# Gate and up projections of a feed-forward block as seven block products, activation kept in DRAM

## Chip, cores and metric

The kernel runs on one core of a Trainium2 chip. The metric is the device time of one launch in microseconds (us). The core has five engines with a queue of their own each, worked through in order: PE (matmuls, with PEld for the weight loads that run beside them), DVE (vector work), ACT (activations and copies), POOL (GpSimd), and SP, whose queue here only issues DMAs.

## What is computed

The program is one encoder layer: three token mixers, an output projection, a SwiGLU feed-forward block and a final norm, for 512 tokens of width 1024. The change touches the seam between output projection and feed-forward, the feed-forward itself, and the start of the down projection:

```python
x = x + merged @ w_out
h2 = rms_norm(x, g_ffn)
ffn = (jax.nn.silu(h2 @ w_ffn_gate) * (h2 @ w_ffn_up)) @ w_ffn_down
return rms_norm(x + ffn, g_final)
```

The gate and up weights are 1024 x 2816 each, the down weight is 2816 x 1024, all in float32.

## The kernel before

**Precision.** A float32 operand is held as a pair: `hi` is the value rounded to the matmul's input type by ACT, `lo` the rest, subtracted out by DVE. `split` does both. `mm3` makes three matmuls of one product: hi by hi, lo by hi, hi by lo. So every operand that a matmul reads costs one pass on ACT and one on DVE first. The DVE pass reads the raw value and `hi`: two inputs in SBUF, unless the raw value still lies in PSUM.

**Weights.** `wload` brings one weight tile of 128 x 1024 by a DMA on SP's queue into `raw` (2 buffers) and splits it into `w_hi` and `w_lo` (3 buffers).

**Seam.** The output projection ends token tile by token tile (four tiles of 128 tokens). After each, `to_h2` scales the normed rows into `xn`, PE transposes them (eight 128 x 128 transposes into two PSUM banks of `pt`, which has 2), and `transpose_split` splits them into `h2_hi`, `h2_lo`: two ACT passes and two DVE passes for each token tile.

**Gate and up.** The loop over `f` has 22 rounds of 128 columns of the feed-forward width. A round loads two tiles, from `w_fg` and `w_fu`, and makes 2 x 8 x 3 matmuls of 512 token columns, gate into a bank of `pg` (2 banks), up into one of `po` (4). The first two rounds are cut into two halves of 256 columns, so that they can begin when the first two token tiles are ready. Then ACT takes the tanh, DVE makes two passes, and a last split writes `act_hi[f]`, `act_lo[f]` in SBUF.

**Down.** `projection` runs over 11 chunks of two `f` for the low half of the output columns, then for the high half, with the tokens as the stationary side and the weights moving.

**Order.** The source is not the order that runs: a scheduler orders each engine's queue by its own model of time when the program is built, and fixes it there. Waits between engines are semaphores. Where a pool of buffers is released and another takes its room, the new tile's first writer waits for the old tile's last users.

Of the kernel before, what the change touches and what calls it, by code (L numbers as in the profile page):

```python
# [55 lines left out]
def block_kernel(ctx, tc, x, mem, pos, inv, g_mix, mem_g, g_ffn, g_final, g_q, g_kv, gate_bias,  # L56
# [37 lines left out]

    def mm3(ps, terms, start=True, stop=True):
        n = len(terms)
        for i, (wh, wl, ah, al) in enumerate(terms):
            mm(ps, wh, ah, start=start and i == 0, stop=False)  # L98
            mm(ps, wh, al, start=False, stop=False)  # L99
            mm(ps, wl, ah, start=False, stop=stop and i == n - 1)  # L100
# [11 lines left out]
    def transpose_split(pp, src, nk, hi, lo, t):  # L112
        for k0 in range(0, nk, 4):
            n = min(4, nk - k0)
            tp = pp.tile([P, 512], F32, name=pp.name, tag=pp.name)
            for k in range(n):
                nc.tensor.transpose(tp[:, k * P:(k + 1) * P], src[:, (k0 + k) * P:(k0 + k + 1) * P], ident)
            tv = tp[:, :n * P].rearrange("p (k c) -> p k c", k=n)
            split(hi[:, k0:k0 + n, t * P:(t + 1) * P], lo[:, k0:k0 + n, t * P:(t + 1) * P], tv)

    with ExitStack() as mix:
# [678 lines left out]
        hp = tc.alloc_tile_pool(name="hp", bufs=1, side="right")  # L800
        gff_b = hp.tile([P, D], F32, name="gff_b")
        bcast_rows(gff_b, g_ffn)
# [31 lines left out]

        def projection(banks, w, nch, tail, ah, al, hold, early, done):
            vs = []
            for half in range(2):
# [31 lines left out]
        def to_h2(t, r):  # L869
            xn = hp.tile([P, D], F32, name="xn", tag="xn", bufs=2)  # L870
# [27 lines left out]
    last = tc.alloc_tile_pool(name="last", bufs=1, side="right")
# [9 lines left out]
    def store(t, r):  # L908
# [4 lines left out]
        for c0 in range(H, D, n):  # L913
# [87 lines left out]
```

## Time and profile before

| what | value |
|---|---|
| time, median of 3 runs | 947.45 us (945.56 to 947.97) |
| profiled execution, span from first to last instruction | 944.7 us |
| PE busy in the span | 927.1 us |
| output projection | up to about 568 us of the span |
| gate and up projection | about 568 to 817 us |
| down projection, final norm and store | about 817 us to the end |

The page gives no time of the profiled execution but its span; the median lies 2.75 us above it. In the timeline a row is start, duration, engine, line, operation, output and inputs, and how many instructions were merged; idle time ahead of it stands in brackets with what ended it. Neighbouring matmuls overlap in these rows, so a matmul's cost is the distance between starts. In the table by stretches each engine has its busy time and its number of instructions, then the clock that PE was granted (1.00 is 2.4 GHz, 0.50 is 1.2 GHz), the DMA engines' share and GB/s.

### The profile page before, as it was taken

The numbers are of one execution on the slowest core, as the hardware profiler recorded it, in microseconds if no ns is written. First come the engines' busy times: TensorE is split into PE (matmuls) and PEld (weight loads), VectorE is DVE, ScalarE is ACT, GpSimd is POOL, SyncE is SP. The second block draws the span as 40 slices with busy tenths as digits, with TensorE's granted clock in tenths as the row PEclk, the third lists the DMA queues.
The fourth block names the chain that finished last, engine by engine and source line by source line (L and its number), as shares of the span: only waits on it lengthen the run. The fifth ranks groups of instructions, "written<-read, shape, count | busy, mean of one in ns | idle before, by whom it ended". The sixth has DMA issues, their size and how long they took to land.

```text
span 944.7 us, 12173 instructions
## 1 busy us (share of the span) xinstructions
PE 927.1 (98%) x4598; PEld 768.6 (81%) x4598; DVE 529.8 (56%) x909; ACT 448.1 (47%) x770; POOL 84.8 (9%) x139
## 2 busy tenths in 40 slices
PE   7998999999999999999999999999999999999997
PEld 5886887888888788888888889888888888888886
DVE  5678968788776756776556664433433334322322
ACT  8566667686653457677664342323222232212222
POOL 2000002212111110100004200000000000000200
PEclk9999999999999999999999999999999999999999
DMA  7521244434332032122225431332223222232222
GB/s 267 157 73 52 74 137 131 150 125 138 134 109 90 26 104 67 56 68 76 76 89 180 133 112 46 100 100 90 90 91 106 94 89 90 90 112 90 93 86 89
DMA packets 32058, 96.32 MB, mean 102 GB/s; under 512 B 4656, under 2 KB 7024, under 8 KB 32000
## 3 DMA queue, kind: packets, MB, share of 16 engines
q1 hardware_dynamic: 29952, 91.25, 29.3%
q0 software_dynamic: 1184, 3.24, 1.0%
q10 hardware_dynamic: 864, 1.06, 0.3%
q8 instruction: 36, 0.59, 0.3%
q14 instruction: 22, 0.18, 0.1%
HBM read 93.36 MB, written 2.18 MB: 101 GB/s over the span
## 4 chain that ended last, share of the span: by engine, by line
PE 87%; DVE 4%; ACT 3%; DMA 3%; issue 2%; POOL 0%; POOLq 0%; DVEq 0%; SPq 0%; ACTq 0%
PE pg L98 17%; PE pg L100 16%; PE pg L99 16%; PE po L98 7%; PE po L100 7%; PE po L99 7%; PE ptp L761 1%; PE psc L98 1%; PE psc L99 1%; PE psc L100 1%; DVE w_lo L80 1%; PE ppv L530 1%; PE ppv L529 1%; PE ppv L531 1%; DMA raw<-w_out_d 1%
## 5 line engine op out<-in xcount | busy, mean ns | idle before, releaser
L79 ACT ACTIVATE w_hi<-raw 128x1024 fp32r<-128x1024 f32 (+3 forms) x150 | 147.3, 984 | 303.0 <-issue 161.1
L80 DVE TENSOR_TENSOR w_lo<-raw,w_hi 128x1024 fp32r<-128x1024 f32 (+3 forms) x150 | 172.5, 1152 | 204.8 <-ACT w_hi L79 203.1
L98 PE MATMUL pg<-h_hi,w_hi 128*128 128x512 f32 (+1 forms) x552 | 215.0, 390 | 0.6 <-DVE q_lo L83 0.6
L99 PE MATMUL pg<-h_lo,w_hi 128*128 128x512 f32 (+1 forms) x552 | 214.6, 389 | 0.0
L100 PE MATMUL pg<-h_hi,w_lo 128*128 128x512 f32 (+1 forms) x552 | 213.9, 388 | 0.0
L100 PEld LDWEIGHTS pg<-h_hi,w_lo 128*128 128x128 f32 x552 | 104.2, 189 | 21.6
L98 PEld LDWEIGHTS pg<-h_hi,w_hi 128*128 128x128 f32 x552 | 104.2, 189 | 21.4 <-DVE q_lo L83 0.8
L99 PEld LDWEIGHTS pg<-h_lo,w_hi 128*128 128x128 f32 x552 | 104.1, 189 | 20.7
L98 PE MATMUL po<-h_hi,w_hi 128*128 128x512 f32 (+1 forms) x192 | 72.9, 380 | 0.0
L100 PE MATMUL po<-h_hi,w_lo 128*128 128x512 f32 (+1 forms) x192 | 72.2, 376 | 0.0
L99 PE MATMUL po<-h_lo,w_hi 128*128 128x512 f32 (+1 forms) x192 | 71.8, 374 | 0.0
L894 DVE TENSOR_TENSOR th<-th,po 128x512 f32<-128x512 f32 x22 | 15.1, 686 | 57.6 <-PE po L100 57.4
L514 ACT ACTIVATE e<-e,ccol 128x512 f32<-128x512 f32 (+3 forms) x64 | 32.5, 554 | 28.3 <-DMA e<-a_dr 27.7
L100 PEld LDWEIGHTS po<-h_hi,w_lo 128*128 128x128 f32 x192 | 36.0, 188 | 7.8
L99 PEld LDWEIGHTS po<-h_lo,w_hi 128*128 128x128 f32 x192 | 36.0, 188 | 7.2
L98 PEld LDWEIGHTS po<-h_hi,w_hi 128*128 128x128 f32 x192 | 36.1, 188 | 6.9
L519 DVE TENSOR_TENSOR e<-e,psc 128x512 f32<-128x512 f32 (+3 forms) x64 | 29.0, 481 | 17.9 <-POOL e L517 14.5
L926 DVE TENSOR_REDUCE nm<-psc 128x1 f32<-128x512 f32 (+1 forms) x48 | 27.7, 596 | 19.9 <-PE psc L100 19.5
L99 PE MATMUL po<-w_lo,act_hi 128*128 128x512 f32 (+1 forms) x104 | 38.8, 373 | 0.0
L98 PE MATMUL po<-w_hi,act_hi 128*128 128x512 f32 (+1 forms) x104 | 38.8, 373 | 0.0
L100 PE MATMUL po<-w_hi,act_lo 128*128 128x512 f32 (+1 forms) x104 | 38.6, 373 | 0.0
L929 ACT ACTIVATE pn<-psc,nm 128x512 f32<-128x512 f32 (+1 forms) x48 | 29.3, 613 | 17.9 <-DVE nm L926 17.9
(428 smaller groups left out, 1729.5 us busy)
## 6 DMA issues: line engine op xcount, KB each, us to landing
raw<-w_zt_d SPq DMA_DIRECT2D x46, 512.0 KB, 3.3
raw<-w_fg_d SPq DMA_DIRECT2D x22, 512.0 KB, 3.2
raw<-w_fu_d SPq DMA_DIRECT2D x22, 512.0 KB, 3.3
raw<-w_fd_d SPq DMA_DIRECT2D x22, 512.0 KB, 3.3
e<-a_dr SPq DMA_DIRECT2D x32, 320.0 KB, 3.5
raw<-w_br_d SPq DMA_DIRECT2D x12, 512.0 KB, 3.3
raw<-w_out_d SPq DMA_DIRECT2D x8, 512.0 KB, 4.2
xt<-x_d SPq DMA_DIRECT2D x4, 512.0 KB, 9.5
```

The costliest lines, as they stand in the source:

```text
L79: A.activation(hi, src, AF.Copy)
L80: V.tensor_tensor(out=lo, in0=src, in1=hi, op=ALU.subtract)
L98: mm(ps, wh, ah, start=start and i == 0, stop=False)
L99: mm(ps, wh, al, start=False, stop=False)
L100: mm(ps, wl, ah, start=False, stop=stop and i == n - 1)
L514: A.activation(e[:, c0:c0 + n], e[:, c0:c0 + n], AF.Exp, bias=ccol[:, j, d, row:row + 1])
L519: V.tensor_tensor(out=e[:, c0:c0 + n], in0=e[:, c0:c0 + n], in1=sc[:, t0:t0 + n], op=ALU.mult)
L529: mm(pv[0:66, t0:t0 + n], vh[:, j, u], s_hi[:, c0:c0 + n], start=first, stop=False)
L530: mm(pv[0:64, t0:t0 + n], vl[:, j, u], s_hi[:, c0:c0 + n], start=False, stop=False)
L894: V.tensor_tensor(out=th, in0=th, in1=pss[1], op=ALU.mult)
L926: nc.vector.tensor_reduce(out=nm, in_=sc, axis=AX.X, op=ALU.max, negate=True)
L929: nc.scalar.activation(pn, sc, AF.Exp, bias=nm, accum_out=sm)
```

## The change

The pair of products `h2 @ w_gate` and `h2 @ w_up` is written as a 2 x 2 block product. The inner width is cut in two halves of four 128-blocks (`KH`), the tokens in two halves of 256 (`HS`). The left blocks of round f are `a11`, `a12` (the two halves of the gate tile) and, from the up tile, its two halves. The right blocks are `b11`, `b21` (first 256 tokens) and `b12`, `b22` (last 256). Strassen's scheme in Winograd's form then needs seven block products in place of eight, on sums of blocks: `s1` to `s4` of the weights, formed anew in each round, and `t1` to `t4` of the activations, formed once at the seam. One product is 4 x 3 matmuls of 256 columns, so a round has 84.

- `lhs_side` loads the two tiles (`raw` and a new `rawb`), forms the four weight sums on GpSimd, 128 x 512 each, and splits 3.5 tiles in place of 2.
- `rhs_side` takes the place of the split in `to_h2`. For tokens 0 to 255 it makes the splits as before and an extra ACT copy of each block. For tokens 256 to 511 it forms `t1`, `t2`, `t3` on DVE and `t4` on GpSimd, and makes five splits for each token tile, where there were two.
- `ffn_first`, `ffn_second`, `ffn_third` are the three parts of a round. Products that share terms go on accumulating in the same bank (`start=False`), and ACT copies of the running sum (`m1`, `u2`, `u4`) are taken in between.
- The activation is no longer split in the loop. It goes to a DRAM tile, `act_dr[f]`. `act_side` reads it back two rounds at a time ahead of each chunk of the down projection's first half (a new argument `prep`), and splits it there.

```diff
+    def rhs_side(pool, dst, raw, t, banks):
+        ...
+        if t < NT // 2:
+            for name, b in zip(("b11", "b21"), banks):
+                raw[name, t] = tmp(f"r{name}", 2)
+                A.activation(raw[name, t], b, AF.Copy)
+                put(name, b)
+            return
+        ...
+        V.tensor_tensor(out=t1, in0=banks[0], in1=b11, op=ALU.subtract)
+        V.tensor_tensor(out=t3, in0=banks[1], in1=b12, op=ALU.subtract)
+        V.tensor_tensor(out=t2, in0=banks[1], in1=t1, op=ALU.subtract)
+        put("b22", banks[1])
+        nc.gpsimd.tensor_tensor(out=t4, in0=b21, in1=t2, op=ALU.subtract)
+        ...
+    def lhs_side(pool, srcs):
+        ...
+        G = nc.gpsimd.tensor_tensor
+        G(out=s12[:, u], in0=b[:, u], in1=b[:, v], op=ALU.add)
+        G(out=s12[:, v], in0=s12[:, u], in1=a[:, u], op=ALU.subtract)
+        G(out=s34[:, u], in0=a[:, u], in1=b[:, u], op=ALU.subtract)
+        G(out=s34[:, v], in0=a[:, v], in1=s12[:, v], op=ALU.subtract)
+        ...
+    def product(ps, lhs, rhs, start=True):
+        (hi, lo), o = lhs
+        mm3(ps, [(hi[:, o + k * P:o + (k + 1) * P], lo[:, o + k * P:o + (k + 1) * P], rhs[0][:, k], rhs[1][:, k])
+                 for k in range(KH)], start=start, more=not start)
...
+    act_dr = dram.tile([NF, P, S], F32, name="act_dr")
+    fg = tc.alloc_tile_pool(name="fg", bufs=1)
...
+    def ffn_first(f):
+        w = lhs_side(fg, (w_fg[f], w_fu[f]))
+        px, py = half(pg), half(po)
+        product(px, w["a11"], h2["b11"])
+        product(py, w["a12"], h2["b21"])
+        m1 = kept(px, "m1")
+        g1 = fg.tile([P, HS], F32, name="g1", tag="g1", bufs=2)
+        V.tensor_tensor(out=g1, in0=py, in1=m1, op=ALU.add)
+        ...
+    def ffn_second(w, px):
+        product(px, w["s2"], h2["t2"], start=False)
+        pz = half(po)
+        product(pz, w["s3"], h2["t3"])
+        u2 = kept(px, "u2")
+        product(px, w["s1"], h2["t1"], start=False)
+        return pz, u2, kept(px, "u4")
+
+    def ffn_third(f, w, px, th, pz, u2, u4):
+        ...
+        V.tensor_tensor(out=u[:, HS:], in0=pz, in1=u4, op=ALU.add)
+        product(px, w["s4"], h2["b22"], start=False)
+        product(pz, w["a22"], h2["t4"], start=False)
+        ...
+        nc.sync.dma_start(out=act_dr[f], in_=u)
...
-    for f in range(NF):
-        pss = []
-        ws = [wload(w[f]) for w in (w_fg, w_fu)]
...
-        split(act_hi[:, f], act_lo[:, f], th, scale=0.5)
...
+    def act_side(c):
+        for f in (2 * c, 2 * c + 1):
+            a = fin.tile([P, S], F32, name="act", tag="act", bufs=4)
+            nc.sync.dma_start(out=a, in_=act_dr[f])
+            split(act_hi[:, f], act_lo[:, f], a, scale=0.5)
```

Three places in the queues. First DVE at the seam, in the kernel before, from the last token tile's residual sum to the last split (`h_lo` is `h2_lo`):

```order
L819 TENSOR_TENSOR x_3_5470<-po,x_3_5470 128x256
L819 TENSOR_TENSOR x_3_5470<-pg,x_3_5470 128x256
L832 TENSOR_SCALAR f_p<-ssx,f_p 128x1
L825 TENSOR_SCALAR f_v<-ssx,f_p 128x1
L80 TENSOR_TENSOR h_lo<-pt,h_hi 128x4x128
L873 SCALAR_TENSOR_TENSOR xn<-x_3_5470,f_r,gff_b 128x512 x2
L80 TENSOR_TENSOR h_lo<-pt,h_hi 128x4x128 x3
```

The same queue with the change, from the split of `b22` for token tile 2 to that of `t3` for token tile 3 (`rt_5913` is `t3`, `rt_5912` is `t2` of tile 3; `s_5939` and `s_6039` are `s1`, `s2` of rounds 0 and 1, `s34r` is `s3`, `s4`):

```order
L84 TENSOR_TENSOR h2b22l<-pt,h2b22h 128x4x128
L84 TENSOR_TENSOR h2t2l<-rt_5817,h2t2h 128x4x128
L977 SCALAR_TENSOR_TENSOR th<-th,g_5989 128x256
L84 TENSOR_TENSOR w_lo<-s_5939,w_hi 128x1024
L84 TENSOR_TENSOR w_lo<-raw,w_hi 128x1024
L146 TENSOR_TENSOR rt_5913<-pt,rb_5909 128x512
L84 TENSOR_TENSOR h2t1l<-rt_5911,h2t1h 128x4x128
L147 TENSOR_TENSOR rt_5912<-pt,rt_5911 128x512
L84 TENSOR_TENSOR h2t4l<-rt_5819,h2t4h 128x4x128
L84 TENSOR_TENSOR s_lo<-s34r,s_hi 128x1024
L84 TENSOR_TENSOR w_lo<-s_6039,w_hi 128x1024
L84 TENSOR_TENSOR h2t3l<-rt_5913,h2t3h 128x4x128
```

The splits of the last two token tiles now stand mixed with weight splits of rounds 0 and 1, and the split of `t3` behind all of them.

Second, DVE in one round of the loop before:

```order
L80 TENSOR_TENSOR w_lo<-raw,w_hi 128x1024
L893 SCALAR_TENSOR_TENSOR th<-th,pg 128x512
L894 TENSOR_TENSOR th<-th,po 128x512
L80 TENSOR_TENSOR w_lo<-raw,w_hi 128x1024
L83 SCALAR_TENSOR_TENSOR act_lo<-th,act_hi 128x512
```

And twelve of the twenty instructions that make a pair of rounds with the change (the scheduler runs the rounds in pairs):

```order
L84 TENSOR_TENSOR w_lo<-s_6825,w_hi 128x1024
L974 TENSOR_TENSOR g_6744<-po,m_6742 128x256
L977 SCALAR_TENSOR_TENSOR th<-th,g_6744 128x256
L84 TENSOR_TENSOR w_lo<-raw,w_hi 128x1024
L974 TENSOR_TENSOR g_6875<-po,m_6873 128x256
L977 SCALAR_TENSOR_TENSOR th<-th,g_6875 128x256
L84 TENSOR_TENSOR w_lo<-s_6956,w_hi 128x1024
L990 TENSOR_TENSOR u<-po,u_6819 128x256
L84 TENSOR_TENSOR w_lo<-raw,w_hi 128x1024
L990 TENSOR_TENSOR u<-po,u_6950 128x256
L84 TENSOR_TENSOR s_lo<-s34r,s_hi 128x1024
L994 SCALAR_TENSOR_TENSOR th<-th,pg 128x256
```

The eight that follow are one more `u<-po`, `a_lo`, `u<-th,u`, `s_lo`, `th<-th,pg`, `u<-po`, `a_lo` and `u<-th,u`, where `a_lo` is the split of the up tile's second half, 128x512, and `u<-th,u` is 128x512. POOL has eight sums of 128x512 for the pair, where it had nothing.

Third, SP's queue around the start of the down projection, in the kernel before:

```order
L88 DMA raw<-w_fg_d 128x1024
L88 DMA raw<-w_fu_d 128x1024
L88 DMA raw<-w_fd_d 128x1024 x22
L916 DMA y_d<-xg_7480 128x512
L916 DMA y_d<-xg_7481 128x512
```

And with the change:

```order
L997 DMA act_dr<-u 128x512
L92 DMA raw<-w_fd_d 128x1024 x2
L997 DMA act_dr<-u 128x512 x2
L92 DMA raw<-w_fd_d 128x1024 x3
L997 DMA act_dr<-u 128x512 x2
L1016 DMA act<-act_dr 128x512 x16
L92 DMA raw<-w_fd_d 128x1024
```

The first load of the activation stands behind the store of rounds 20 and 21 in this queue, and its semaphores make it wait for both stores to land.

## Rows read from the trace of the kernel before

**Rows 1.** Page, part 1: busy us, share of span, instructions of each engine.

```profile
PE 927.1 (98%) x4598; PEld 768.6 (81%) x4598; DVE 529.8 (56%) x909; ACT 448.1 (47%) x770; POOL 84.8 (9%) x139
```

**Rows 2.** Table by stretches, 100 us of the gate and up loop.

```profile
600.00:700.00 100.00, 100.00 (x430) 80.42 (x430) 38.80 (x45) 27.32 (x36) 0.00 (x0) 1.00 0.29 95
```

**Rows 3.** Timeline of PE: loop matmuls of 512 columns, then 256 columns, one weight load.

```profile
700.16 0.40 PE L98 MATMUL po<-h_hi,w_hi 128*128 128x512 f32 x1
...
704.83 0.39 PE L100 MATMUL po<-h_hi,w_lo 128*128 128x512 f32 x1
...
577.95 0.28 PE L99 MATMUL pg<-h_lo,w_hi 128*128 128x256 f32 x1
577.96 0.19 PEld L100 LDWEIGHTS pg<-h_hi,w_lo 128*128 128x128 f32 x1
...
579.15 0.28 PE L98 MATMUL pg<-h_hi,w_hi 128*128 128x256 f32 x1
```

**Rows 4.** Timeline of POOL and DVE, 510 to 518 us, and two DVE splits later.

```profile
510.15 2.55 POOL L186 TENSOR_TENSOR merged<-merged,th_o_hi 128x512 f32<-128x512 f32 x2 [10.03 <-DVE th_o_hi L185]
512.67 4.50 POOL L186 TENSOR_TENSOR merged<-merged,th_o_hi 128x512 f32<-128x512 f32 x2
...
510.52 1.28 DVE L185 SCALAR_TENSOR_TENSOR th_o_hi<-th_o_hi,psc 128x512 f32<-128x512 f32 x2
511.71 4.31 DVE L80 TENSOR_TENSOR w_lo<-raw,w_hi 128x1024 fp32r<-128x1024 f32 x2
515.95 1.77 DVE L83 SCALAR_TENSOR_TENSOR mg_lo<-merged,mg_hi 128x512 fp32r<-128x512 f32 x1
...
529.27 2.35 DVE L80 TENSOR_TENSOR w_lo<-raw,w_hi 128x1024 fp32r<-128x1024 f32 x2
```

**Rows 5.** Groups by line, shapes apart: count, busy us, mean ns, idle before.

```profile
L80 DVE TENSOR_TENSOR w_lo<-raw,w_hi 128x1024 fp32r<-128x1024 f32 x41 | 50.2, 1224 | 84.5 <-ACT w_hi L79 84.5
L83 DVE SCALAR_TENSOR_TENSOR act_lo<-th,act_hi 128x512 fp32r<-128x512 f32 x20 | 13.7, 684 | 0.0
L819 DVE TENSOR_TENSOR x<-po,x 128x256 f32<-128x256 f32 x2 | 0.8, 420 | 0.6 <-PE po L100 0.6
L79 ACT ACTIVATE w_hi<-raw 128x1024 fp32r<-128x1024 f32 x41 | 43.5, 1061 | 163.6 <-issue 146.8 <-PE pg L99 16.8
```

**Rows 6.** Timeline of DVE and PE at the seam.

```profile
569.83 0.21 DVE L825 TENSOR_SCALAR f_v<-ssx,f_p 128x1 f32<-128x1 f32 x1 [0.19 <-ACT junk L821]
...
576.50 0.69 DVE L80 TENSOR_TENSOR h_lo<-pt,h_hi 128x512 fp32r<-128x512 f32 x1 [0.71 <-ACT h_hi L79]
...
568.27 0.28 PE L98 MATMUL pg<-h_hi,w_hi 128*128 128x256 f32 x1
...
575.23 0.60 PE L117 MATMUL pt<-ident,xn 128*128 128x128 f32 x4
```

**Rows 7.** DMA issues: output and input, queue, count, KB each, us to landing.

```profile
raw<-w_fu_d SPq DMA_DIRECT2D x22, 512.0 KB, 3.3
...
y_d<-xg SPq DMA_DIRECT2D x3, 256.0 KB, 2.6
...
raw<-w_uv_d SPq DMA_DIRECT2D x2, 256.0 KB, 2.6
```

**Rows 8.** Timeline of PE at the start of the down projection.

```profile
816.83 0.39 PE L100 MATMUL po<-h_hi,w_lo 128*128 128x512 f32 x1
...
817.07 0.39 PE L98 MATMUL po<-w_hi,act_hi 128*128 128x512 f32 x1
```

**Rows 9.** Table by stretches around an idle PE, and the timeline's idle time there.

```profile
78.40 0.38 PE L98 MATMUL psc<-k_hi,q_hi 128*128 128x256 f32 x1 [2.00 <-ACT pn L929]
...
75.50:77.90 2.40, 0.90 (x6) 0.52 (x4) 1.85 (x5) 0.12 (x1) 0.00 (x0) 1.00 0.00 1
77.90:81.35 3.45, 2.34 (x8) 1.80 (x9) 3.29 (x9) 3.45 (x9) 1.04 (x2) 0.80 0.02 4
81.35:85.00 3.65, 3.65 (x15) 2.96 (x14) 3.56 (x7) 1.21 (x4) 0.00 (x0) 0.72 0.43 144
```

More of the change, by code (lines that the diff above doesn't have):

```diff
@@ L93, in wload, with mm3 @@
         return hi, lo
[L95 removed]
+    def mm3(ps, terms, start=True, stop=True, more=False):
         n = len(terms)
         for i, (wh, wl, ah, al) in enumerate(terms):
[L98 to L100 removed]
+            mm(ps, wh, ah, start=start and i == 0, stop=False, skip_group_check=more)
+            mm(ps, wh, al, start=False, stop=False, skip_group_check=more)
+            mm(ps, wl, ah, start=False, stop=stop and i == n - 1, skip_group_check=more)
     def bank(pool):
@@ new lines, in lhs_side, with both @@
+    def lhs_side(pool, srcs):
+        a = stage.tile([P, 1024], F32, name="raw", tag="raw", bufs=2)
+        b = pool.tile([P, 1024], F32, name="rawb", tag="rawb", bufs=2)
+        for raw, src in zip((a, b), srcs):
+            nc.sync.dma_start(out=raw, in_=src)
+        u, v = slice(0, 512), slice(512, 1024)
+        s12, s34 = (pool.tile([P, 1024], F32, name=n, tag=n, bufs=2) for n in ("s12", "s34r"))
+        G = nc.gpsimd.tensor_tensor
[3 more added lines that the diff above has]
+        G(out=s34[:, v], in0=a[:, v], in1=s12[:, v], op=ALU.subtract)
+        def both(src, n=1024, tag=None):
+            hi, lo = ((pool if tag else stage).tile([P, n], F32R, name=nm, tag=nm, bufs=2 if tag else 3)
+                      for nm in ((f"{tag}_hi", f"{tag}_lo") if tag else ("w_hi", "w_lo")))
+            split(hi, lo, src)
+            return hi, lo
+        w = both(a)
+        m = {"a11": (w, 0), "a12": (w, 512)}
+        w = both(s12)
+        m |= {"s1": (w, 0), "s2": (w, 512)}
+        w = both(s34, tag="s34")
+        m |= {"s3": (w, 0), "s4": (w, 512)}
+        m["a22"] = (both(b[:, v], 512, "a22"), 0)
+        return m
@@ L800, in block_kernel @@
         hp = tc.alloc_tile_pool(name="hp", bufs=1, side="right")
-        gff_b = hp.tile([P, D], F32, name="gff_b")
+        h2 = {n: [hp.tile([P, KH, HS], F32R, name=f"h2{n}{i}") for i in "hl"] for n in RHS}
+        hx = tc.alloc_tile_pool(name="hx", bufs=1, side="right")
+        gff_b = hx.tile([P, D], F32, name="gff_b")
         bcast_rows(gff_b, g_ffn)
@@ L833, in partial, with projection @@
             return v
-        def projection(banks, w, nch, tail, ah, al, hold, early, done):
+        def projection(banks, w, nch, tail, ah, al, hold, early, done, prep=None):
             vs = []
@@ L842, in projection @@
                 for c in range(lead):
+                    if prep and half == 0:
+                        prep(c)
                     wc = wload(w[half, c])
@@ new lines, in to_h2, with half, kept @@
+            rhs_side(hx, h2, h2_raw, t, banks)
+        projection(((po,) * 4, (po,) * 3, (po, pg)), w_out, 4, 4, mg_hi, mg_lo, hold_out, lambda t: None, to_h2)
+        hx.release()
+    act_dr = dram.tile([NF, P, S], F32, name="act_dr")
+    fg = tc.alloc_tile_pool(name="fg", bufs=1)
+    def half(pool):
+        return bank(pool)[:, :HS]
+    def kept(src, name):
+        t = fg.tile([P, HS], F32, name=name, tag=name, bufs=2)
+        A.activation(t, src, AF.Copy)
+        return t
+    def ffn_first(f):
[6 more added lines that the diff above has]
+        V.tensor_tensor(out=g1, in0=py, in1=m1, op=ALU.add)
+        th = fg.tile([P, S], F32, name="th", tag="th", bufs=2)
+        A.activation(th[:, :HS], g1, AF.Tanh, scale=0.5)
+        V.scalar_tensor_tensor(out=th[:, :HS], in0=th[:, :HS], scalar=1.0, in1=g1, op0=ALU.add, op1=ALU.mult)
+        return w, px, th
@@ L878, in block_kernel @@
+    nxt = ffn_first(0)
+    for f in range(NF):
+        w, px, th = nxt
+        second = ffn_second(w, px)
+        if f + 1 < NF:
+            nxt = ffn_first(f + 1)
+        ffn_third(f, w, px, th, *second)
+    fg.release()
+    hp.release()
     fin = ctx.enter_context(tc.tile_pool(name="fin", bufs=1))
```

48 lines of the change are left out of this document (31 added, 17 removed).

## Prediction, made before the changed kernel was run

> **What bounds the kernel now.** I read the page's busy times first, then the table by stretches for the loop, then the timelines at the loop's two ends, because the change works there. PE is busy for 98% of the span [rows 1], and in the gate and up loop for 100 us of 100, with DVE at 38.8, ACT at 27.3 and POOL at nothing [rows 2]. So the loop lasts as long as its matmuls. What one costs is the distance between starts, not the row's duration: twenty steps of 512 columns take 704.83 - 700.16 = 4.67 us, or 0.2335 each, and ten of 256 columns 579.15 - 577.95 = 1.20, or 0.120 each [rows 3]. A round of 48 is 11.2 us, each of the first two, in halves, 96 x 0.120 = 11.5, and the loop 20 x 11.2 + 2 x 11.5 = 247.2 us. PE crosses both of its ends without a stop: the loop's first matmul starts at 568.27 while the last token tile is still being normed [rows 6], and the down projection's first follows the loop's last by 0.24 us [rows 8].
>
> **The seven products.** 22 rounds of 84 matmuls at 0.120 are 221.8 us, so PE's work falls by 25.4 us. That is 10%, not an eighth, since two steps of 256 columns cost 0.240 against 0.2335. A weight load of 0.19 us starts 0.01 after the matmul ahead of it, and the steps stay at 0.120 [rows 3]: the loads are covered. The Trainium skill (TensorE: Matmul & The Clock Gate, The mechanism) says that a weight load overlaps with matmuls in flight only when the two use different row groups; here both use all rows. By that rule nothing would be covered, which is the third rival below; the trace does not agree.
>
> **DVE and GpSimd take turns.** The change puts eight GpSimd sums of 128x512 into a pair of rounds, beside DVE passes that mostly read two operands in SBUF. Such neighbours stand in the trace already [rows 4]. While DVE worked from PSUM (the pair at 510.52), two POOL sums took 2.55 us. Then DVE's two weight splits took 4.31, against 2.35 for the two at 529.27 with POOL idle. The sums line up end to end: POOL's second ends at 510.15 + 2.55 = 512.70, the fourth at 512.67 + 4.50 = 517.17; DVE's splits end at 511.71 + 4.31 = 516.02, and its next one, of 512, at 517.72. So the fourth POOL sum has 517.17 - 516.02 = 1.15 us to itself, the small split 0.55, and what lies between 512.70 and 516.02 is one more sum and two big splits of (3.32 - 1.15) / 2 = 1.09. They never ran together. The Trainium skill states this as a rule (SBUF — State Buffer, Who interferes with whom): a DVE instruction with two SBUF inputs and a GpSimd one that reads SBUF lock each other out for a whole instruction. By that rule the sum is the one below; if the rows were chance, it would be the first rival's.
>
> **The loop, pair by pair.** PE needs 168 x 0.120 = 20.2 us. What must take turns: POOL 8 x 1.15 = 9.2, DVE six splits of 1024 at 1.09, four passes of 512 at 0.55 and two of 256 at about 0.3 (half of 0.55), 9.3 together: 18.5 us. Eight more DVE passes read PSUM, at 0.42 each [rows 5], 3.4 in all. Under a POOL sum they are free, and in the queue's order six stand where POOL has a sum to run; two stand where it waits for `rawb` to be reloaded. That makes 18.5 + 0.8 = 19.3 against 20.2, so PE still sets the pace, with 0.9 to spare. POOL's own circle is as tight: reload 3.3 [rows 7], eight sums 9.2, some 6 us of DVE turns between them, an ACT pass of 1.06 [rows 5], 19.6. ACT has some 12 of 20 us. With three engines at 95% and every order fixed, I take 0.4 us of PE waits for a pair, 4 us for ten pairs (the first is in the seam). The ends are 0, and 18.5 + 3.4 - 20.2 = 1.7 for a pair, 17 us, if nothing is hidden.
>
> **The seam.** All second products need sums over token tiles 2 and 3. In DVE's queue the split of `t3` for tile 3 is the gate: PE has `t3` products at its head then, and before them only 48 matmuls of rounds 0 and 1 (5.8 us) and the last 16 transposes (about 1.5). DVE reaches the last `f_v` at 569.8 as before [rows 6]. Behind it, up to that split, stand 17 passes of 512, four weight splits of 1024 and two passes of 256. With POOL silent that is 17 x 0.62 + 4 x 1.18 + 0.8 = 16 us (0.62 between 0.55 and the 0.68 of rows 5; 1.18 is half of 2.35), and the gate opens at 586. But `rawb` lies in room that the output projection's operands held, so its first load starts when that ends, at 568.3, and lands 3.3 later [rows 7], at 571.6. From then on POOL has 13 sums queued (rounds 0 and 1, three of round 2, both `t4`), 15 us, and DVE's two-input passes must fit between them: eight of 512, four of 1024 and a few rests, 9.4 us. The passes from PSUM hide under POOL. So the gate opens at 571.6 + 15 + 9.4 = 596. PE idles for 596 - 568.3 - 5.8 - 1.5 = 20 us. The ends are 11 (POOL costs nothing, from 586 with a little for hops), and 24 (1.28 for a sum, as in the pair of 2.55, and 1.18 for a split). I take 20, since that is the very pair of instructions [rows 4].
>
> **Through DRAM.** After the loop's last matmul come an add from PSUM 0.42, a product of 512 at 0.6, the store, the load behind it on SP's queue, which waits for the store to land, and an ACT pass of 0.6, before the down projection's first matmul. Stores and loads of 256 KB land in 2.6 each [rows 7]: 6.8, with hops 7 us where there was 0.24. The ends are 6 and 9. Later chunks hide: two loads, 1.2 us of ACT and 1.4 of DVE beside 24 matmuls of 512 columns.
>
> **The clock.** After 2.0 us without work PE was granted 0.80 of full speed for 3.45 us and 0.72 for 3.65 [rows 9]; part of that was at 1.2 GHz. This cost 0.69 + 1.02 = 1.7 us. I count it once after each of the two stops, 3.4; the ends are 0 and 7.
>
> **The sum.** -25.4 + 20 + 4 + 7 + 3.4 = +9.0. The span of 944.7 becomes 953.7, and with the 2.75 by which the median lies above that span, **956.5 us**.
>
> **Rivals.** *First, faster: the turns cost little at the seam.* If DVE's critical passes go ahead of the weight sums, or the two overlap after all, the stop is 11 and the loop adds nothing: -25.4 + 11 + 7 + 3.4 = -4.0, 943.5 us. It decides below a stop of about 13 us. For it: POOL spans are rough, and these rows hold only a few sums [rows 4]. Against it: their ends fit to 0.1 us. *Second, slower still: DVE and GpSimd become the loop's bound.* This happens once a pair needs more than PE's 20.2 us, so when more than four of the eight PSUM passes stay uncovered. With none covered it costs 17 in place of 4: 969.5; short waits on PE at half clock would take it to some 978. For it: the 0.9 us to spare, and an order made without the turns. Against it: PE is some 2 to 3 us ahead of DVE where the queue's order couples them. *Third, weight loads show.* If each load of 0.19 [rows 3] stood alone, 1848 x 0.19 adds 351: 1308 us. The covered loads speak against it [rows 3]. That the change does less than it says is no case, since the matmuls are counted in the queue.
>
> **How the numbers follow.** Forecast 0.60 (950 to 963), first rival 0.18, second 0.20, third and anything else 0.02. The range 943 to 972 leaves out about half of the first rival and a third of the second. This kernel's measurement tells 0.3%, 2.8 us, from no change. Faster: most of the first rival, 0.11. Same: its rest and the forecast's lower edge, 0.13. Slower: 0.76.
>
> **What would show it.** In the timeline PE stops between about 572 and 596 us, but for one burst, with DVE's splits of 2 us beside POOL sums; DVE's mean for 128x1024 in the loop rises from 1.22 to about 2. A pair of rounds takes 20.2 to 21 us. PE stops for 7 us ahead of the down projection, its releaser an ACT pass that waited for a DMA of `act`. PEclk falls below 1 after each stop. I am wrong if PE's stop at the seam is under 13 us, if a pair takes over 21.5, or if the steps of 256 columns are not 0.120.

## The result, and the profile after

The changed kernel takes 953.67 us (median of four runs, 952.62 to 954.92), the kernel before 946.91 in the same comparison: a ratio of 1.0074, with a 95% interval of 1.0055 to 1.0093. The forecast was 956.5, slower. The profiled execution spans 951.3 us against 944.7, 6.6 more, and that difference is what the sections below take apart.

The page of the changed kernel: busy time of each engine, and in the slices of 23.8 us PE, POOL and the granted clock.

```profile
PE 909.5 (96%) x5294; PEld 792.9 (83%) x5294; DVE 642.9 (68%) x1053; ACT 515.9 (54%) x914; POOL 240.2 (25%) x229
...
PE   7998999999999999999999993999999999799997
...
POOL 2000002212112110010004108467765674000200
PEclk9999999999999999999999996899999999899999
```

PE is busy 17.6 us less than before, with 696 matmuls and transposes more [rows 1]. There is one hole in slice 25, the seam, and a small one in slice 35, the loop's other end; the clock falls in and behind both. POOL works where it stood idle. The table by stretches (us: busy time and count of PE, PEld, DVE, ACT, POOL; granted clock, DMA share, GB/s) tells the same:

```profile
572.00:584.00 12.00, 2.25 (x13) 1.72 (x11) 12.00 (x13) 7.79 (x12) 11.88 (x8) 0.69 0.31 112
584.00:600.00 16.00, 8.93 (x44) 8.60 (x45) 16.00 (x13) 5.70 (x9) 13.73 (x8) 0.61 0.20 65
...
660.00:780.00 120.00, 120.00 (x1002) 120.00 (x1002) 97.17 (x119) 62.90 (x108) 82.38 (x48) 1.00 0.40 127
...
800.00:820.00 20.00, 14.54 (x120) 14.26 (x119) 10.45 (x17) 6.19 (x12) 0.00 (x0) 0.97 0.43 132
820.00:840.00 20.00, 18.37 (x73) 15.06 (x74) 12.61 (x18) 11.84 (x18) 0.00 (x0) 0.86 0.78 251
```

In the middle of the loop PE never waits, as before [rows 2]; DVE has gone from 38.8 of 100 us to 97 of 120 and POOL from nothing to 82. All that is lost is lost at the two ends. First the seam, as the timeline has it: PE's stops (the bracket: idle time ahead of the row, and what ended it), and DVE and POOL ahead of the last of them.

```profile
579.63 1.11 PE L949 MATMUL pt<-ident,xn 128*128 128x128 f32 x4 [6.92 <-DVE rt L145]
...
586.68 0.58 PE L104 MATMUL pg<-h2b11h,w_lo 128*128 128x256 f32 x1 [5.52 <-DVE w_lo L84]
...
596.17 0.58 PE L103 MATMUL po<-h2t3l,s_hi 128*128 128x256 f32 x1 [4.38 <-DVE h2t3l L84]
...
589.93 2.31 DVE L84 TENSOR_TENSOR s_lo<-s34r,s_hi 128x1024 fp32r<-128x1024 f32 x1
592.17 2.28 DVE L84 TENSOR_TENSOR w_lo<-s,w_hi 128x1024 fp32r<-128x1024 f32 x1
594.37 1.74 DVE L84 TENSOR_TENSOR h2t3l<-rt,h2t3h 128x512 fp32r<-128x512 f32 x1
...
591.12 2.25 POOL L149 TENSOR_TENSOR rt<-rb,rt 128x512 f32<-128x512 f32 x1
593.33 2.24 POOL L166 TENSOR_TENSOR s34r<-raw,rawb 128x512 f32<-128x512 f32 x1
```

The prediction named the gate, DVE's split of `t3` for token tile 3, and put its end at 596; it ends at 596.1. PE stands still for 6.92 + 5.52 + 4.38 = 16.8 us. A DVE split of 1024 columns that took 1.22 [rows 5] takes 2.3 here, a POOL sum 2.2 in place of 1.28 [rows 4]. Then the loop's end: PE's last and next matmul, DVE's last product, the SP queue, and the ACT pass that PE waits for.

```profile
814.26 0.28 PE L104 MATMUL po<-h2t4h,a_lo 128*128 128x256 f32 x1
821.63 0.77 PE L102 MATMUL po<-w_hi,act_hi 128*128 128x512 f32 x1 [7.09 <-ACT act_hi L86]
...
815.04 0.69 DVE L996 TENSOR_TENSOR u<-th,u 128x512 f32<-128x512 f32 x1
...
814.32 1.76 SPq L997 DMA_DIRECT2D act_dr<-u  x2
817.93 11.49 SPq L1016 DMA_DIRECT2D act<-act_dr  x12
...
820.90 1.15 ACT L86 ACTIVATE act_hi<-act 128x512 fp32r<-128x512 f32 x2 [8.81 <-DMA act<-act_dr]
```

PE waits 7.09 us where it had followed on after 0.24 [rows 8]: product until 815.73, store until the first load is issued at 817.93, load until 820.90, ACT, PE. What follows starts slowly: the first twelve of the down projection's matmuls start within 826.13 - 821.63 = 4.50 us, where eleven steps of 0.227 are 2.50. The granted clock of that stretch, and of three at the seam, is 0.50, the 1.2 GHz level:

```profile
821.60:825.60 4.00, 3.97 (x9) 3.13 (x10) 2.60 (x5) 2.38 (x5) 0.00 (x0) 0.50 0.66 216
579.60:581.00 1.40, 1.37 (x6) 1.25 (x6) 1.40 (x2) 0.63 (x1) 1.40 (x2) 0.50 0.00 0
586.70:590.00 3.30, 3.30 (x15) 3.30 (x16) 3.30 (x5) 1.62 (x3) 3.30 (x3) 0.50 0.00 0
596.20:600.20 4.00, 4.00 (x19) 4.00 (x20) 4.00 (x4) 0.00 (x0) 2.84 (x3) 0.50 0.00 0
```

The first loop matmul starts between 566.7 and 570.3 us in the kernels below, though the work ahead of it is nearly the same; so I compare the stretch from there to the down projection's first matmul, and the rest after it. Before: 248.80 and 127.63. Changed: 253.27 and 129.67, which is 4.47 and 2.04 of the 6.6 us. Each ratio below is to the kernel before as it ran beside that kernel (medians of 945.97 to 946.91 us).

| kernel | median us | ratio to before (95%) | stretch | rest | stops at the seam | stop ahead of down |
|---|---|---|---|---|---|---|
| before | 946.91 | | 248.80 | 127.63 | 0 | 0 |
| changed | 953.67 | 1.0074 (1.0055 to 1.0093) | 253.27 | 129.67 | 16.8 | 7.09 |
| e1, no weight sums | 945.03 | 0.9985 (0.9970 to 1.0000) | 244.84 | 129.40 | 8.4 | 6.87 |
| e3, two plain rounds | 945.54 | 0.9991 (0.9978 to 1.0005) | 243.96 | 130.14 | 4.0 | 6.83 |
| e5, two chunks early | 951.23 | 1.0046 (1.0033 to 1.0059) | 250.30 | 130.31 | 16.6 | 4.29 |
| e9, last store aside | 948.94 | 1.0035 (1.0021 to 1.0048) | 250.03 | 127.84 | 16.4 | 2.84 |
| e10, plain, late sums | 934.17 | 0.9882 (0.9856 to 0.9908) | 236.30 | 128.45 | 3.5 | 2.39 |

### The profile page after: what moved, and what is told of

The parts are those of the page before. It is cut to its first block, busy times and chain, and to the rows that moved or that the text cites. A ratio compares the mean times of both kernels' runs of the same rounds, so it can differ in the third digit from the quotient of the medians.

```text
span 951.3 us, 14138 instructions
## 1 busy us (share of the span) xinstructions
PE 909.5 (96%) x5294; PEld 792.9 (83%) x5294; DVE 642.9 (68%) x1053; ACT 515.9 (54%) x914; POOL 240.2 (25%) x229
## 4 chain that ended last, share of the span: by engine, by line
PE 80%; DVE 7%; DMA 5%; issue 3%; ACT 2%; POOL 1%; SPq 0%; POOLq 0%; DVEq 0%; ACTq 0%
PE pg L102 16%; PE pg L104 16%; PE pg L103 15%; PE po L102 6%; PE po L103 6%; PE po L104 6%; DVE w_lo L84 2%; PE ptp L829 1%; PE psc L102 1%; PE psc L103 1%; PE psc L104 1%; DMA e<-a_dr 1%; DMA xt<-x_d 1%; DMA raw<-w_out_d 1%; PE ppv L598 1%
## 5 line engine op out<-in xcount | busy, mean ns | idle before, releaser
L102 PE MATMUL pg<-h_hi,w_hi 128*128 128x512 f32 x360 | 142.2, 396 | 1.0 <-DVE q_lo L87 0.6
L103 PE MATMUL pg<-h_lo,w_hi 128*128 128x512 f32 x360 | 142.5, 396 | 0.0
L104 PE MATMUL pg<-h_hi,w_lo 128*128 128x512 f32 x360 | 142.0, 395 | 0.1
L102 PEld LDWEIGHTS pg<-h_hi,w_hi 128*128 128x128 f32 x360 | 67.9, 189 | 15.2 <-ACT w_hi L83 0.8
L104 PEld LDWEIGHTS pg<-h_hi,w_lo 128*128 128x128 f32 x360 | 68.1, 189 | 14.4 <-DVE w_lo L84 0.5
L103 PEld LDWEIGHTS pg<-h_lo,w_hi 128*128 128x128 f32 x360 | 67.9, 189 | 13.4
L164 POOL TENSOR_TENSOR s<-rawb 128x512 f32<-128x512 f32 x22 | 33.8, 1535 | 68.2 <-DMA rawb<-w_fu_d 61.2
L165 POOL TENSOR_TENSOR s<-s,raw 128x512 f32<-128x512 f32 x22 | 43.8, 1990 | 0.0
L167 POOL TENSOR_TENSOR s34r<-raw,s 128x512 f32<-128x512 f32 x22 | 40.0, 1816 | 0.8
L166 POOL TENSOR_TENSOR s34r<-raw,rawb 128x512 f32<-128x512 f32 x22 | 37.4, 1698 | 1.2 <-DVE s_lo L84 1.2
```

What stands on the lines that cost most here:

```text
L102: mm(ps, wh, ah, start=start and i == 0, stop=False, skip_group_check=more)
L103: mm(ps, wh, al, start=False, stop=False, skip_group_check=more)
L104: mm(ps, wl, ah, start=False, stop=stop and i == n - 1, skip_group_check=more)
L164: G(out=s12[:, u], in0=b[:, u], in1=b[:, v], op=ALU.add)
L165: G(out=s12[:, v], in0=s12[:, u], in1=a[:, u], op=ALU.subtract)
L166: G(out=s34[:, u], in0=a[:, u], in1=b[:, u], op=ALU.subtract)
```

## The experiments

**The weight sums left out (e1).** What is at stake is why DVE is late at the seam.

```diff
-        G(out=s12[:, u], in0=b[:, u], in1=b[:, v], op=ALU.add)
...
-        G(out=s34[:, v], in0=a[:, v], in1=s12[:, v], op=ALU.subtract)
+        s12, s34 = b, a
```

> Left out: the four GpSimd sums of each round (88 in all); the raw weight blocks are split and multiplied in their place, so PE, ACT and DVE have the same passes and matmuls as in the changed kernel, and only the two t4 sums of the token side stay on GpSimd. The changed kernel stood still on PE for 6.92 + 5.52 + 4.38 = 16.8 us at the seam, its DVE splits of 128x1024 took 1.47 to 1.90 us in the loop. Theory (DVE and GpSimd take turns): the splits fall to 1.22, the pass that gates the second products (t3 of token tile 3) has 17 passes of 512, three of 1024 and two of 256 ahead of it from 569.8, about 15 us, so it ends near 585 in place of 596; PE stops for 7 to 10 us in all, and with the shorter half-clock stretch the span falls by 8 to 11, to 940 to 943. Rival (turns cost little, the order of DVE's queue or the late weight loads set the stop): the stop stays above 13 us and the span within 4 us of 951.3. In the loop itself both expect no change, since PE sets its pace.

Measured: the stops are 2.29 + 0.25 + 1.82 + 1.47 + 2.60 = 8.4 us. The last ends at 587.3, with ACT's pass on `t3`; DVE's split of `t3`, expected near 585, ends at 589.4: from 570.76 on five weight splits of 1024 stand ahead of it, where three were counted. The stretch falls by 8.43, the span to 943.7, 0.7 above the expected range, since the loop began 1.1 us later. The groups of DVE from 600 to 780 us (count, busy us, mean ns, idle before), first of the changed kernel, then of this one:

```profile
L84 DVE TENSOR_TENSOR w_lo<-raw,w_hi 128x1024 fp32r<-128x1024 f32 x18 | 34.6, 1924 | 7.3 <-ACT w_hi L83 7.2
L84 DVE TENSOR_TENSOR s_lo<-s34r,s_hi 128x1024 fp32r<-128x1024 f32 x19 | 29.5, 1554 | 0.9 <-ACT s_hi L83 0.9
L84 DVE TENSOR_TENSOR w_lo<-s,w_hi 128x1024 fp32r<-128x1024 f32 x18 | 26.6, 1480 | 18.1 <-ACT w_hi L83 18.1
...
L994 DVE SCALAR_TENSOR_TENSOR th<-th,pg 128x256 f32<-128x256 f32 x18 | 7.3, 408 | 0.0
```

```profile
L84 DVE TENSOR_TENSOR w_lo<-rawb,w_hi 128x1024 fp32r<-128x1024 f32 x18 | 22.1, 1226 | 41.8 <-ACT w_hi L83 41.8
L84 DVE TENSOR_TENSOR w_lo<-raw,w_hi 128x1024 fp32r<-128x1024 f32 x18 | 22.1, 1225 | 15.0 <-ACT w_hi L83 15.0
L84 DVE TENSOR_TENSOR s_lo<-raw,s_hi 128x1024 fp32r<-128x1024 f32 x18 | 21.9, 1219 | 0.9 <-ACT s_hi L83 0.9
```

Splits with both operands in SBUF fall from 1.48 to 1.92 us back to 1.22; the pass that reads PSUM stood at 0.41 either way. So the turns are real. The Trainium skill (SBUF — State Buffer, Who interferes with whom) gives the turns as a rule for just these operands; here the trace agrees with it.

How much of the seam's stop the turns are, e1 alone can't tell. Without the weight sums the scheduler also ordered DVE's queue anew. And turns are not wholly gone: of the two `t4` sums that are left, one lasts 6.66 us beside DVE's passes, against 1.28 alone:

```profile
577.31 6.66 POOL L149 TENSOR_TENSOR rt<-rb,rt 128x512 f32<-128x512 f32 x1 [3.37 <-DVE rt L147]
```

The changed kernel's own rows price the turns without a change of order. DVE has no idle time there from 572 to 600, in the table above. Between 574.20 and 596.04 it makes twelve passes with both operands in SBUF, in 19.4 us. At the distances that e1 shows for such passes undisturbed (0.60 us for 512 columns, 1.13 for 1024, 0.34 for 256) they would take 7 x 0.60 + 4 x 1.13 + 0.34 = 9.1. So by this estimate the turns held the gate back by about 10 us, well over half of the stop. The rest is passes in DVE's own queue, which the rival had named, and in e1 two of the five stops end with a pass on ACT.

**One GpSimd sum more in each round (e6).** This asks how near the loop's middle is to the turns.

```diff
+        G(out=extra, in0=b[:, u], in1=b[:, v], op=ALU.add)
```

> The changed kernel with one more GpSimd sum of 128x512 in every round (into a tile that nobody reads). The prediction's sum for a pair of rounds was 18.5 us of DVE and GpSimd in turns and 0.8 uncovered against 20.2 of PE. If that holds, two more sums in a pair make it 21.6, GpSimd and DVE set the pace, and the loop grows by about 1.4 us a pair, 14 us in all (10 to 18), span 961 to 969. If the turns take less than was summed, PE keeps the pace, pairs stay at 20.2 and the span stays within 4 us of 951.3, the seam's stop growing by some 3 us at most.

The table by stretches of the loop's middle, and PE's stops, one in each pair of rounds:

```profile
660.00:780.00 120.00, 117.31 (x950) 114.55 (x949) 118.04 (x113) 60.22 (x102) 100.71 (x57) 1.00 0.36 122
...
664.48 0.39 PE L104 MATMUL po<-h2b21h,w_lo 128*128 128x256 f32 x1 [0.44 <-DVE w_lo L84]
...
685.86 0.39 PE L104 MATMUL po<-h2b21h,w_lo 128*128 128x256 f32 x1 [0.42 <-DVE w_lo L84]
...
707.06 0.39 PE L104 MATMUL po<-h2b21h,w_lo 128*128 128x256 f32 x1 [0.44 <-DVE w_lo L84]
```

DVE is now busy, or waiting for its turn, for 118 of 120 us, and a pair takes 21.2 (685.86 to 707.06) where it took 20.16. The sum of the prediction gave 21.6. Taking the two sums of 1.15 off, a pair of the changed kernel needs 21.2 - 2.3 = 18.9 of turns: PE has 1.3 us in hand, not 0.9. The time is 972.51 us, 1.0273 of before (1.0249 to 1.0296). The span rose by 17.7, more than ten pairs cost (10.5), for a reason that had nothing to do with sums; e2 met it first.

**Activation of the first chunk kept in SBUF (e2).** Rounds 0 and 1 write `first[f]`, in 8 KB a partition that are taken ahead of the loop's pool `fg`, and chunk 0 of the down projection reads them.

```diff
+    pre = ctx.enter_context(tc.tile_pool(name="pre", bufs=1))
+    first = [[pre.tile([P, S], F32R, name=f"fa{f}{i}") for i in range(2)] for f in range(2)]
     fg = tc.alloc_tile_pool(name="fg", bufs=1)
...
+        if f < 2:
+            split(first[f][0], first[f][1], u, scale=0.5)
+        else:
+            nc.sync.dma_start(out=act_dr[f], in_=u)
```

> The activation of rounds 0 and 1 is split straight into two pairs of SBUF tiles and never goes through DRAM; the other 20 rounds are as in the changed kernel, and the down projection's first weight chunk reads those tiles. In the changed kernel PE stood still for 7.09 us ahead of the down projection, and its first nine or ten matmuls then came 0.427 us apart in place of 0.227. Theory (store, load and ACT pass of the last rounds are on the path): the stop falls to under 1 us, the half clock there goes, the span falls by 7 + 1.8 = 8.8, to 942.5. Rival (the path only moves to the second chunk, whose loads also start when the loop ends): a stop of 2 to 5 us appears 5.4 us into the down projection, and the span falls by 3 to 6, to 945 to 948.

It took 959.24 us, 1.0135 of before (1.0103 to 1.0168), and missed twice. The `rawb` loads in SP's queue, in the changed kernel and in this one:

```profile
568.55 11.91 SPq L160 DMA_DIRECT2D rawb<-w_fu_d  x4
```

```profile
584.87 12.05 SPq L160 DMA_DIRECT2D rawb<-w_fu_d  x4
...
594.22 0.58 PE L102 MATMUL pg<-h2t2h,w_hi 128*128 128x256 f32 x1 [15.41 <-ACT w_hi L83]
...
833.84 0.77 PE L102 MATMUL po<-w_hi,act_hi 128*128 128x512 f32 x1 [4.56 <-ACT act_hi L86]
```

Taking 8 KB made the weight loads come 16 us later. So did 2 KB more inside `fg` (e6: first load at 581.35, 13 us later, PE's stop 16.32) and 1 KB ahead of it (e7: 584.72, 15.11). What the first load waited for stands in the waits of SP's queue (us in total, times, longest), in the changed kernel and in e2; e6 and e7 have the same row as e2:

```profile
SPq L160 <- PE pg L104: 23.5, 1, 23.5
```

```profile
SPq L160 <- DVE h2t4l L84: 37.9, 1, 37.9
```

In the changed kernel it is the output projection's last matmul. In the other three it is DVE's split of `t4` for token tile 3, the last pass on the token sums, and the load is issued 0.06 to 0.07 us after that pass ends. I read it thus: `fg` lies in the room of the output projection's operands and fills it; any more reaches into the tiles in which the seam forms its token sums. The traces show the wait, not the addresses. The other miss: the chunk that was ready ran ahead of the loop's last products (its first matmul at 812.58, the loop's last at 826.82), so it covered nothing, and 4.56 us of stop stood ahead of chunk 1, which still came through DRAM. The rival's 2 to 5 us.

**Matmuls in the gap (e7).** This prices the clock alone.

```diff
+    for i in range(52):
+        mm(wp[:, :HS], wm[:, :P], wm, start=True, stop=True)
     fg.release()
```

> The changed kernel with 52 matmuls of 256 columns between the loop and the down projection, on one small tile that ACT makes from the last round's result; nobody reads what they give, and they take 52 x 0.120 = 6.2 us of the 7.09 for which PE stood still there. Theory (part of the price of the stop is TensorE's lower clock after it): the down projection's first matmuls then come 0.227 us apart at once, in place of 0.427 for the first nine, and the time from the loop's last matmul to the down projection's 26th falls by 1.6 to 2.0 us. If the slow start had another cause, such as weights or activations that come late, the first matmuls stay 0.4 apart.

```profile
823.55 6.40 PE L1012 MATMUL pt<-wm 128*128 128x256 f32 x52
...
830.59 0.47 PE L102 MATMUL po<-w_hi,act_hi 128*128 128x512 f32 x1 [0.64 <-issue]
830.90 0.40 PE L103 MATMUL po<-w_lo,act_hi 128*128 128x512 f32 x1
```

The first twelve starts now span 833.19 - 830.59 = 2.60 us in place of 4.50, and from the loop's last matmul to the down projection's 26th the time falls by 2.1 us, from 15.05 to 12.92. So 1.9 us of the rest's 2.04 are the lower clock at which PE came out of its stop; here it was granted 1.00 from 830.6 on. (The 960.86 us of this kernel, 1.0150 of before, are those of its late weight loads.)

**What the load behind the loop waits for (e5, e9).** In e5 chunks 0 and 1 are loaded into `raw` tiles of the weight ring, which no pool of the loop covers; in e9 chunk 0 alone, and the last two rounds' products go to tiles of another pool and are stored from there.

```diff
+        if c < 2:        # e9: 1
+            held = stage.tile([P, 1024], F32, name="raw", tag="raw", bufs=2)
...
-        V.tensor_tensor(out=u, in0=th, in1=u, op=ALU.mult)
-        nc.sync.dma_start(out=act_dr[f], in_=u)
+        v = keep.tile([P, H], F32, name="junk", tag="junk", bufs=2) if f >= NF - 2 else u   # e9
+        V.tensor_tensor(out=v, in0=th, in1=u, op=ALU.mult)
+        nc.sync.dma_start(out=act_dr[f], in_=v)
```

> The changed kernel, with the activation of the down projection's first two weight chunks (rounds 0 to 3) loaded into the weight ring's raw tiles, which no pool of the loop covers, in place of tiles that lie where the loop's own tiles lay. In the changed kernel the first load of the activation could be issued only when the last stores had left (817.9 us, loop's last matmul at 814.3), and PE stood still for 7.09 us. Theory (the 7 us are store, load and ACT pass behind the loop's end, as summed in the prediction; what the load waits for is room): with the data already in SBUF only an ACT pass of 0.6 and its hops stay, the stop is 0.5 to 1.5 us, the half clock at the start of the down projection goes, and from the loop's first matmul to the down projection's 26th the time falls by 7 to 8.5; span 943 to 945. Rival (the next chunks come late, as when the first chunk alone was in SBUF): a stop of 2 to 5 us two chunks on, span 946 to 949.

> The changed kernel, with the first two rounds' activation loaded ahead into one raw tile of the weight ring (as above, but for one chunk), and the last two rounds' results written by DVE into tiles outside the loop's room, from where they are stored. With two chunks loaded ahead the stop ahead of the down projection was 4.29 us: the ACT pass had its data since about 809, but it stood until 818.57, when the last store had read its tile, since what the pass writes lies where that tile lay. Theory (the stop is room that comes free: first by the last store, and without that by the last DVE product at 815.7): the ACT pass starts some 0.2 to 0.5 us after that product, PE some 0.8 later, the stop is 1.7 to 2.8 us in place of 7.09, the span 945 to 948. Rival (the wait is for the data, store to load through DRAM): the stop stays between 4 and 7 us.

ACT and PE of e5, then DVE, ACT and PE of e9:

```profile
818.57 2.19 ACT L86 ACTIVATE act_hi<-raw 128x512 fp32r<-128x512 f32 x4 [4.58 <-DMA act_dr<-u]
...
819.29 0.77 PE L102 MATMUL po<-w_hi,act_hi 128*128 128x512 f32 x1 [4.29 <-ACT act_hi L86]
```

```profile
817.28 0.69 DVE L997 TENSOR_TENSOR junk<-th,u 128x512 f32<-128x512 f32 x1
...
818.13 1.15 ACT L86 ACTIVATE act_hi<-raw 128x512 fp32r<-128x512 f32 x2 [2.69 <-DVE junk L997]
...
818.86 0.47 PE L102 MATMUL po<-w_hi,act_hi 128*128 128x512 f32 x1 [2.84 <-issue]
```

In e5 the data was in SBUF (its load was issued at 805.58), and ACT still waited until the last store had read `u`: 4.29 us of stop, where I had expected 0.5 to 1.5. The theory of e5 was right on the load and blind to the pass behind it: by what ended its wait, `act_hi` too lies where `u` lay. In e9 ACT follows the last product by 0.16 us, and 2.84 us are left, 0.04 above the range, because DVE put a weight split ahead of that product. So the store is on the path because it is the last to read the loop's room, and the load because it can't be issued before; the data itself is not late. Both together cost 7.09 - 2.84 = 4.3 us of stop, and in e9 the clock stayed up as well (the rest: 127.84).

**Two plain rounds (e3, e4, e8, e10, e11).** Rounds 0 and 1 as eight block products, first token half, then second; rounds 2 to 21 as changed. Room for `b12` comes from three smaller buffers. e4 adds the edit of e2, e8 that of e5; e11 adds one chunk loaded early and the last product aside, e10 the same and loads round 1's weights into the `rawb` tiles.

```diff
-    nxt = ffn_first(0)
-    for f in range(NF):
+    for f in range(2):
+        ffn_plain(f)
+    nxt = ffn_first(2)
+    for f in range(2, NF):
...
+        if f == 1:       # e10
+            rb = [fg.tile([P, 1024], F32, name="rawb", tag="rawb", bufs=2) for _ in range(2)]
```

> Rounds 0 and 1 are made as eight block products in the order first token half, then second (no weight sums, no token sums); rounds 2 to 21 keep the seven products. Theory: the seam's stop is due to the second products wanting the token sums of tiles 2 and 3, and GpSimd's sums, too early; two plain rounds give DVE and GpSimd 23 us of PE work in place of the 48 matmuls and cost 2 x 12 x 0.120 = 2.9 us of PE. The stop of 16.8 and the half clock around it (some 45 matmuls by 0.213 in place of 0.120, 4.2 us) go: span 951.3 - 16.8 - 4.2 + 2.9 = 933. Rival (the stop only moves to round 2): PE stops for 5 to 15 us near 592, span 938 to 948.

> Both of these edits in one kernel: two plain rounds, and their activation kept in SBUF. If the two stops are independent the gains add: 951.3 - 18.1 - 8.8 = 924.5 us of span, about 2% under the kernel before. If one stop's cover depends on the other, or the rivals above hold, it lies between 932 and 945.

> Two plain rounds, as in the run with these alone, and the first two chunks of the activation loaded early, as above. The plain rounds took 9.3 us from the stretch between the loop's first and the down projection's first matmul (253.27 to 243.96) and left 6.83 of the stop ahead of the down projection. If that stop goes too, with its half clock, the span is 944.4 - 6 - 1.8 = 936.5 (934 to 939), 1% under the kernel before. If it comes back at a later chunk, 940 to 943.

> As the run before, without the move of round 1's weights. Theory: the seam as in the first run with plain rounds (4 us of stops), the stop ahead of the down projection 2 to 3 us in place of 6.83: from the loop's first to the down projection's first matmul 243.96 - 4.3 = 239.7 (238.5 to 241), span 938 to 941.

> Two plain rounds, round 1's weights loaded into the two rawb tiles, so that GpSimd's first weight sums come some 5 us later than in the run with plain rounds alone and DVE's passes on token tiles 2 and 3 have SBUF to themselves for longer; and the end of the loop as in the run above (one chunk ahead, the last round's result outside the loop's room). Theory: of the 4.0 us of stops that the plain rounds left at the seam about half goes, the stop ahead of the down projection is 2 to 3 us: from the loop's first to the down projection's first matmul 243.96 - 2 - 4.5 = 237.5 (236 to 239), span 936 to 939. Rival (round 1's weights, loaded only from 568, come late): PE waits 2 to 5 us for a split near 580 and the stretch is 240 to 242.

In e3 the stretch fell by 9.3, not 18. Of the stops 4.0 us stayed (PE waits for DVE, whose passes on token tile 2 still stand beside six sums), some 1.8 of half clock with them, and 2.8 of small waits came up later in the loop and at its end; the two plain rounds cost the 2.9 of matmuls that were expected. e4 (942.71 us, 0.9966) kept a stop of 4.5 at chunk 1, as e2 did; its gains did not add. Its first `rawb` load, too, waited for the split of `t4`, until 584.89. So its weight sums came after DVE's passes on the token tiles, the only stop at the seam was 0.55, and the clock stayed at 1.00 from 568 to 600; waits of 4.6 us came behind, from 598 to 615. e8 (944.92 us, 0.9981) had 4.24 ahead of the down projection as e5 did, and a further 2.92 at a weight chunk, whose load had waited while the second activation chunk held its `raw` tile. e11 (940.36 us, 0.9940) has the stretch that was expected, 239.96, but a stop of 3.56 in place of 2 to 3.

e10 is the fastest: 934.17 us, 0.9882 of before. Its stops:

```profile
583.07 0.39 PE L102 MATMUL pg<-h2b22h,w_hi 128*128 128x256 f32 x1 [1.05 <-ACT h2b22h L83]
585.91 0.39 PE L103 MATMUL pg<-h2b22l,w_hi 128*128 128x256 f32 x1 [2.23 <-DVE h2b22l L84]
...
803.15 0.47 PE L102 MATMUL po<-w_hi,act_hi 128*128 128x512 f32 x1 [2.39 <-issue]
```

The stretch, 236.30, lies in the expected range, and the span, 931.6, below its range of 936 to 939. But the reason given for half of it was wrong: the seam's stops are 3.5 us, where e3 has 4.0 and e11 3.2. Against e11 the 3.7 us are a shorter stop at the end (2.39 for 3.56; in e11 a weight split of 1.23 us stands on DVE ahead of the last round's product, in e10 behind it), about 1 us of small waits in rounds 2 to 5 that are gone, and less half clock at the seam. Another 2.6 lie behind the loop, where e11 came out of its stop at the lower clock and e10 did not, and 2.2 ahead of it, in the start that scatters between all these kernels. How much the move of round 1's weights did to each of these is not settled.

## Why the prediction was right, and where its sizes were off

- **PE's own work, -25.4: as summed.** Matmuls of 256 columns come 0.120 apart; the first `s4` product of one pair starts at 648.06, of the next at 668.22 and 688.38: 20.16 us for 168. No weight load shows, so the third rival is out.
- **The seam, 20: the gate right, the stop 16.8.** DVE opened the gate at 596.1, as summed from turns: 13 sums and 12 passes with both operands in SBUF, as the trace has them. What the sum missed is that the matmuls and transposes ahead of the gate do not run in one go at full speed: they fill 27.8 - 16.8 = 11.0 us between 568.36 and 596.17, not 7.3, because PE was halted three times and came back at half clock. The prediction had one burst; so the stop was too long and the clock too cheap, in part by the same microseconds. e1 bears out the turns (without the weight sums 8.4), and so do the 10 us that DVE's passes took longer in the changed kernel. The upper end of 24 is not what its own prices give: 13 x 0.13 and 4 x 0.09 us more than the sum for 20 make 22.
- **Pairs of rounds, 4: mis-sized, 0.3.** The working (19.3 of turns against 20.2) was near what e6 shows (18.9), but from a margin of 0.9 the prediction added 0.4 of waits for each pair on no row at all. DVE's mean for a 1024 split was 1.65, not about 2. With 1.3 in hand and the same order in every pair, PE waits for nothing from 600 to 780. The second rival fell with it; that it was close is e6's finding, since one more sum in a round makes DVE the bound.
- **Through DRAM, 7: 7.09, with a reason left out.** Store, load and ACT pass are on the path in the order given. But the prediction let the load wait for the store without asking for what; e5 and e9 show that it is room and not data, since the rows it reads were written long before. Nor did it see that the ACT pass waits for that room as well.
- **The clock, 3.4: too low, about 6.** At the seam, from rows at either spacing, 15 steps of 0.225 and 19 of 0.222 in place of 0.120 and a few shorter pieces cost 4.2 us; ahead of the down projection it is 2.0, and e7 gives 1.9 back. The price of 1.7 from [rows 9] was that of a stop of 2 us.
- **The sum.** -25.4 + 16.8 + 0.3 + 6.85 + 6.2 = +4.8, measured +6.6. Of the rest 0.7 is the way idle time is counted, from a row's modelled end 0.28 after its start where the next could have come after 0.120, at four stops. Some 1.1 us I cannot place. That the forecast came within 2.8 us of the measured time is in part luck: the seam (3.2 too much) and the pairs (3.7 too much) erred one way, the clock (2.8 too little) and what I cannot place the other. With the pairs or the clock mended alone the forecast would have been 952.8 or 959.3.
- **The first rival** (turns cost little, 943.5) decided below a stop of 13 us. Its condition was not met: the stop is 16.8. In e1, where only the two `t4` sums take turns, the stop is 8.4 and the time 945.03. That this is near its price is chance in part, since its stop of 11 was too long and its 3.4 for the clock too little: in e1 the clock stood at 0.50 from 575.4 to 592.5.

## What to carry to other kernels

A faster inner loop is judged at its ends: this one saved 25 us of TensorE work in the middle and lost 32, nearly all of it at the two places where the pipeline fills and drains. With two plain rounds ahead of it, one chunk loaded early and the last store taken aside the kernel came out 6 us under the one before (e11), and with round 1's weights moved as well 12 (e10); what the last step did is not settled. When work is put on GpSimd, count DVE's passes with two SBUF operands and the sums as one engine, in each stretch and not over the span. Ask of each transfer behind a loop what it waits for, data or room: where a pool fills its room exactly, the next kilobyte can hold back the loads behind it, here by 13 to 16 us; the spans of e2 and e7 are 7 to 8 us longer than the changed kernel's.

## What the hardware showed that I had not expected

- Ahead of the down projection, after stops of 2.84 us (e9) and 2.39 (e10), PE went on with a granted clock of 1.00 (2.4 GHz); after 3.56 (e11), 4.29 (e5) and 7.09 it came back at 0.50 for 4 to 5.4 us. The length of a stop does not decide it alone. At the seam of e10 a stop of 2.23 us, 1.05 us of idle time not long before it, was followed by 0.50 from 586.5 on, and in the kernel before a stop of 2.00 behind 2.4 us with little work by 0.80 [rows 9]. The first of these rows is e9's, the next two are e10's (down projection, then seam), the last is e5's.

```profile
818.90:823.00 4.10, 4.10 (x18) 3.40 (x19) 1.19 (x2) 0.84 (x2) 0.00 (x0) 1.00 0.94 330
```

```profile
803.20:807.20 4.00, 4.00 (x18) 3.31 (x19) 2.49 (x4) 1.01 (x2) 0.06 (x1) 1.00 0.84 271
```

```profile
586.50:589.90 3.40, 3.40 (x19) 3.40 (x18) 3.40 (x3) 1.54 (x2) 3.40 (x2) 0.50 0.02 5
```

```profile
819.30:823.70 4.40, 4.40 (x11) 3.43 (x11) 3.73 (x6) 3.12 (x6) 0.00 (x0) 0.50 0.91 287
```

- The taking of turns stretches both sides: a POOL sum of 1.28 alone stands at 1.7 or 2.2 beside DVE's splits, a split of 1.22 at 2.3, while DVE's passes from PSUM stay at 0.41 beside the same sums.
